# A decoder layer in single-precision split matmuls: how far weights are split ahead, where the gate job stands, how the first chunks and the last job are cut

## The chip, the core and the metric

The kernel runs on one core of a Trainium2 chip. A core has a matrix engine (TensorE, PE in the profile; its weight loads are shown apart as PEld), a vector engine (DVE), a scalar engine (ACT), a general engine (POOL) and SyncE (SP), which here issues nearly all transfers. Each engine works through its own list in order; semaphores hold an instruction until what it reads has been written. Accumulation goes to PSUM, everything else lies in SBUF, and transfers (DMA) run on 16 DMA engines. The metric is the device time of one execution in microseconds (us).

## The reference, cut to what matters

One decoder layer over 256 prompt tokens and 64 sample tokens (8 sequences of 8), 320 columns in all, with a model width of 2048:

```python
x = x + 0.5 * swiglu(rmsnorm(x, ln_ffa), w_ffa_in, w_ffa_out)      # d_ff 5632
x = x + token_mixer(rmsnorm(x, ln_mix), ...)
x = x + 0.5 * swiglu(rmsnorm(x, ln_ffb), w_ffb_in, w_ffb_out)
y = rmsnorm(x, ln_f)
# token_mixer: one projection h @ w_in gives mLSTM q/k (conv + SiLU), v, output gate, input/forget
# gates (8 columns: mif), attention q, k, v, and two branch gates;
# out = (sigmoid(gm) * (hm @ w_pm) + sigmoid(ga) * (ha @ w_pa)) @ w_out
```

`hm` is the mLSTM (chunked, with a running-max stabiliser) and `ha` the dilated attention over a cache of 2048 positions for the sample tokens. New keys, values and states are outputs too.

## The kernel before, in words

Activations are held transposed: a pair tile is 128 partitions x 2 x 320 columns, and eight pairs make one x. Each float32 operand of a large product is split into a high part, rounded to the matmul's format, and a low part, the rest. A product is three matmuls into the same PSUM tile: high weight x high activation, high weight x low activation, low weight x high activation.

The work is a list of jobs (`add_job`). A job makes 256 output columns and is cut into chunks of up to four 128-row blocks of the weight, 512 KB each; a full chunk is 2 halves of the columns x 4 blocks x 3 = 24 matmuls of 320 columns. There are 784 weight chunks and one gate chunk (`mif`, 16 blocks of 8 columns). A weight chunk goes through three steps: `load_upto` issues its transfer into one of RAWB raw buffers on SP; `split_upto` has ACT write the high part (`hi`, L223) and DVE the low part (`lo`, L224), into one of HLB pairs of buffers; PE uses it (L144, PSUM tile `fg`, two buffers). In chunk ci the kernel before splits up to chunk ci+2 (HLB 3) and issues loads up to chunk ci+6 (HLB + RAWB = 7 ahead, exclusive).

`run_job` (L270 on) writes the order of all engines out by hand. For each chunk: transfers that were put off (`run_later`), the split, then one step of each background generator (`even` and `odd` in alternate chunks, `slow` at 8 steps in 15 chunks, `every` in each), then, in a job's first chunk, its `setup` and `flush_evac`, which reads out the PSUM tile of the job before; then the loads, then the matmuls. Background generators are the attention over prompt (`prompt_attention`, even) and cache (`sample_attention`, slow), the `mlstm` (odd), the later parts of evacuations (every). Their small matmuls go to PSUM tile `bg` (four buffers) and stand in the PE list between chunks.

Stages: the first SwiGLU; the mixer projection: for p = 0..3 a job each for attention q, k, v, then `mif`, then per head mLSTM v (`mv`), two q/k jobs (`qk_evac`) and the output gate, then 16 gate jobs; then 8 jobs of `w_pm`, 8 of `w_pa`, 8 of `w_out`; the second SwiGLU. `mif_evac` (L801 on) computes log-sigmoids, scans and exponentials of 4-row tiles in nine steps of one chunk each. `mv_evac` scales its PSUM tile by rstd (L395) and two chunks later transposes it on PE (L332). `mlstm` loads q and k of head h+1 (`load_head`) after the fourth of four state steps of head h. The activations of `w_pm` (`hr`) and `w_pa` (`ar`) are four pair tiles; `presplit` splits the first of them during the job before, and `take` the others when the first job starts (L1301, L1302).

At the start, x is loaded in four quarters of 512 columns and transposed on PE; `first_chunk` and `prep_pair` put these transposes, the gains (L1469) and the low parts (L1473) of two pairs ahead of, or between, the halves of the first chunks; `warm(8)` is filler matmuls. At the end, the last job is read out in `ffb_last`, squares are summed over rows by matmuls against ones (`token_sums`), the final norm's scale is made (L1582 to L1584), and Y is scaled in two halves of 1024 columns and stored by six transfers from SP.

Of the kernel before, what the change touches and what calls it, by code (L numbers as in the profile page):

```python
# [128 lines left out]
def decoder_kernel(tc, I, O, K):  # L129
# [55 lines left out]
    RAWB, HLB, KRB = 4, 3, 3  # L185
# [219 lines left out]
    xl = {}  # L405

    def load_x(c):
        xl[c] = fp.tile([128, 3, 512], F32, tag="xl", bufs=3, name="xl")
        G.memset(xl[c][64:128, 2], 0.0)
        dma(xl[c][:, 0:2], I["x_prompt"][0].rearrange("(t p) d -> p t d", p=128)[:, :, c * 512:(c + 1) * 512])  # L410
        dma(xl[c][0:NS, 2], I["x_sample"].rearrange("b t d -> (b t) d")[:, c * 512:(c + 1) * 512])
# [194 lines left out]
    def sample_attention():  # L606
# [145 lines left out]
        for u in range(17):  # L752
# [51 lines left out]
    def mif_evac(ps):  # L804
# [5 lines left out]
        rst = mp_tile("rst")[0:4, :, 0:NT]  # L810
# [156 lines left out]
    def mlstm():  # L967
# [313 lines left out]
    add_job(w_in, 0, 16, C_MIF, mov_x, mif_evac, kind="mif")  # L1281
# [25 lines left out]
    def presplit(key):  # L1307
        while key not in M:
            yield
        PRE[key] = split_act(M[key][0], t_tile)  # L1310

    def take(key):
        for h in range(4):
            BH[h], BL[h] = PRE[key] if h == 0 and key in PRE else split_act(M[key][h], t_tile)
# [83 lines left out]
    def token_sums(x):  # L1398
        ps = bg_tile()
        for t, t0 in enumerate(TOK):  # L1400
            for m in range(2):
                mm(ps[:, t:t + 1], x[:, m, t0:t0 + 128], ones[:, 0:1], m == 0, m == 1)
        return ps


    def ffb_last(ps, j):
# [3 lines left out]
        if j < 7:  # L1410
            V.scalar_tensor_tensor(X[j], ps[:, :, 0:NT], 0.5, X[j], op0=OP.mult, op1=OP.add)
            sumsq(X[j], j, p)
        else:
            Y["sq"] = ft_tile("sq")
            for m in range(2):
                V.scalar_tensor_tensor(X[j][:, m], ps[:, m, 0:NT], 0.5, X[j][:, m], op0=OP.mult, op1=OP.add)
                S.activation(Y["sq"][:, m], X[j][:, m], AF.Square)
# [5 lines left out]
        if j < 7:  # L1423
            yield
        if j == 6:
            pa_ = token_sums(state["ss"])
            V.tensor_copy(rt, pa_[:, 0:3])
# [25 lines left out]
    vps = bg_tile()  # L1453
    tr(vps[:, 0:16], vffa)
    V.tensor_copy(gv[:, 0:16], vps[:, 0:16])

    def prep_pair(j, fg=False):
# [3 lines left out]
        ft = fg_tile() if fg else None  # L1461
        ps = [ft[:, 0], ft[:, 1]] if fg else [bg_tile(), bg_tile()]
# [4 lines left out]
        V.tensor_copy(X[j][:, 1], ps[1][:, 0:NT])  # L1467
        for m in range(2):
            S.activation(XH[j][:, m], ps[m][:, 0:NT], AF.Copy, scale=gv[:, g0 + m:g0 + m + 1])  # L1469
            if m == 0:  # L1470
                S.copy(X[j][:, 0], ps[0][:, 0:NT])
# [4 lines left out]
    def first_chunk(n, m):  # L1476
        if n == 0 and m == 0:
# [5 lines left out]
        elif n < 3:  # L1483
            prep_pair(2 * n + 2 + m)
            if m == 1:
                split_upto(n + 2)
        elif m == 0:
            split_upto(n + 2)

    def vec_table():  # L1490
        for _ in range(4):
# [6 lines left out]
    def first_sumsq():  # L1498
        for c in ((), (), (0,), (1, 2), (3, 4, 5), (6, 7)):
# [3 lines left out]
        rstd_now()  # L1503

    def init_tables():
        yield
# [68 lines left out]
    for job in jobs:  # L1575
        run_job(job)
    run_later()


    flush_evac()  # L1580
    pb_ = token_sums(Y["sq"])
    V.tensor_tensor(rt, rt, pb_[:, 0:3], op=OP.add)  # L1582
# [5 lines left out]
    for c in range(2):  # L1588
        if c:
            drain()  # L1590
        for t in range(3):
            r0 = 0 if t < 2 else 64
            a = yt[r0:128, t, c * 1024:(c + 1) * 1024]
            if t == 1:
                S.activation(a, a, AF.Copy, scale=rt[r0:128, t:t + 1])
            else:
                V.tensor_scalar(a, a, rt[r0:128, t:t + 1], None, op0=OP.mult)  # L1597
            dma((ypv[:, t] if t < 2 else ysv)[:, c * 1024:(c + 1) * 1024], a)
# [34 lines left out]
```

## Time and profile before

| | |
|---|---|
| median of 3 runs | 2980.31 us (2979.14 to 2981.5) |
| profiled execution's own time | 2975.59 us |
| its span, first to last instruction | 2973.8 us |
| PE busy | 2924.8 us (98%) |
| DVE / ACT / POOL busy | 1637.5 / 1087.8 / 226.0 us |
| read from and written to memory | 521.58 MB, 32.28 MB |

The span covers the instructions; the profiled time is 1.8 us more. A matmul's end is modelled, so the PE's busy time holds a little pipeline overlap. Windows give busy time for stretches of the span, with the clock that was granted to TensorE (1.00 is full speed) and the mean share of the DMA engines; waits name the instruction or transfer that ended an engine's idle time.

### The profile page before, as it was taken

The page shows a single profiled execution, that of the slowest core. Times are in us where ns is not written, and L with a number is a line of the kernel's source. Part 1 is how long each engine was busy: PE and PEld are TensorE (multiplying, and loading weights), DVE is VectorE, ACT ScalarE, POOL GpSimd, SP SyncE. Part 2 cuts the span into 40 slices and gives each one's busy share as a digit, 9 for nine tenths or more (in the row PEclk, how much of TensorE's full clock was granted, in tenths as well). Part 3 has the DMA queues.
Part 4 walks back from the last instruction along what each step waited for, and adds up shares of the span by engine and source line. Part 5 has one row for each costly group of instructions (what it writes and reads, how often), then busy time and mean ns, then how long its engine had stood idle before and what let it go on. Part 6 is the DMA issues. An engine that isn't in the chain of part 4 may idle for free.

```text
span 2973.8 us, 51323 instructions
## 1 busy us (share of the span) xinstructions
PE 2924.8 (98%) x21538; PEld 2875.4 (97%) x21538; DVE 1637.5 (55%) x1939; ACT 1087.8 (37%) x1359; POOL 226.0 (8%) x256
## 2 busy tenths in 40 slices
PE   9999999999999999999999999999999999999998
PEld 8999999999999999988889999999999999999998
DVE  6444444444446556878888875654444444444444
ACT  5332333333334333433443443334333333333334
POOL 1000000000000000122222210000000000000000
PEclk9999999999999999999999999999999999999999
DMA  6454444444546788898999986554444444445443
GB/s 195 151 159 155 149 149 149 149 150 143 158 145 184 224 231 248 223 296 272 301 282 313 308 275 218 184 176 152 150 149 149 149 149 150 151 146 156 149 141 115
DMA packets 507477, 557.23 MB, mean 187 GB/s; under 512 B 30125, under 2 KB 452061, under 8 KB 507221
## 3 DMA queue, kind: packets, MB, share of 16 engines
q1 hardware_dynamic: 507068, 553.87, 61.2%
q8 instruction: 169, 2.77, 0.4%
q14 instruction: 64, 0.52, 0.1%
q10 hardware_dynamic: 176, 0.07, 0.0%
HBM read 521.58 MB, written 32.28 MB: 186 GB/s over the span
## 4 chain that ended last, share of the span: by engine, by line
PE 50%; DMA 1%; DVE 1%; issue 0%; ACT 0%; DVEq 0%; SPq 0%; ACTq 0%
PE fg L144 47%; PE bg L144 3%; PE bg L332 0%; DMA raw<-in_w_in_dram 0%; DMA vt<-in_cache_v_dram 0%; DMA k<-qk_d 0%; DMA raw<-in_w_pm_dram 0%; DVE kd L631 0%; DVE lo L224 0%; DVE pre L928 0%; ACT hi L223 0%; DVE sg L958 0%; DVE vs L1073 0%; DVE Y L1597 0%; DVE bl L1302 0%
## 5 line engine op out<-in xcount | busy, mean ns | idle before, releaser
L224 DVE TENSOR_TENSOR lo<-raw,hi 128x1024 fp32r<-128x1024 f32 (+1 forms) x784 | 969.1, 1237 | 1204.2 <-ACT hi L223 1189.9
L144 PE MATMUL fg<-xh,hi 128*128 128x320 f32 x4240 | 1323.0, 312 | 2.6 <-ACT hi L223 2.6
L144 PE MATMUL fg<-xh,lo 128*128 128x320 f32 x4240 | 1314.3, 310 | 8.6 <-DVE lo L224 8.6
L144 PE MATMUL fg<-xl,hi 128*128 128x320 f32 x4240 | 1313.0, 310 | 0.0
L223 ACT CAST hi<-raw 128x1024 fp32r<-128x1024 f32 (+1 forms) x784 | 806.3, 1029 | 1356.7 <-PE fg L144 1014.2
L144 PEld LDWEIGHTS fg<-xh,lo 128*128 128x128 f32 x4240 | 797.4, 188 | 11.7 <-DVE lo L224 11.5
L144 PEld LDWEIGHTS fg<-xh,hi 128*128 128x128 f32 x4240 | 797.9, 188 | 5.7 <-ACT hi L223 3.1
L144 PEld LDWEIGHTS fg<-xl,hi 128*128 128x128 f32 x4240 | 797.8, 188 | 1.0 <-issue 0.2
L144 PE MATMUL fg<-hh,hi 128*128 128x320 f32 x1408 | 437.0, 310 | 0.0
L144 PE MATMUL fg<-hl,hi 128*128 128x320 f32 x1408 | 435.2, 309 | 0.0
L144 PE MATMUL fg<-hh,lo 128*128 128x320 f32 x1408 | 435.2, 309 | 0.0
L144 PEld LDWEIGHTS fg<-hl,hi 128*128 128x128 f32 x1408 | 264.4, 188 | 0.7 <-issue 0.7
L144 PEld LDWEIGHTS fg<-hh,hi 128*128 128x128 f32 x1408 | 264.4, 188 | 0.7 <-issue 0.7
L144 PEld LDWEIGHTS fg<-hh,lo 128*128 128x128 f32 x1408 | 264.4, 188 | 0.0
L439 POOL TENSOR_TENSOR gt<-gt,rstd 128x640 f32<-128x640 f32 x44 | 69.2, 1573 | 1876.8 <-ACT gt L438 1876.8
L144 PE MATMUL fg<-bl,hi 128*128 128x320 f32 x512 | 158.5, 310 | 1.9 <-DVE bl L1302 1.9
L144 PE MATMUL fg<-bh,hi 128*128 128x320 f32 x512 | 158.7, 310 | 1.5 <-ACT bh L1301 1.5
L144 PE MATMUL fg<-bh,lo 128*128 128x320 f32 x512 | 158.3, 309 | 0.0
L631 DVE STREAM_TRANSPOSE kd<-kraw 128x512 f32<-128x512 f32 x160 | 101.2, 677 | 10.8 <-DMA kraw<-in_cache_k_dram 10.8
L144 PEld LDWEIGHTS fg<-bl,hi 128*128 128x128 f32 x512 | 96.1, 188 | 2.4 <-DVE bl L1302 2.4
L144 PEld LDWEIGHTS fg<-bh,hi 128*128 128x128 f32 x512 | 96.1, 188 | 2.2 <-ACT bh L1301 2.0
L144 PEld LDWEIGHTS fg<-bh,lo 128*128 128x128 f32 x512 | 96.1, 188 | 0.0
(295 smaller groups left out, 1495.7 us busy)
## 6 DMA issues: line engine op xcount, KB each, us to landing
raw<-in_w_ffa_in_dram SPq DMA_DIRECT2D x176, 512.0 KB
raw<-in_w_in_dram SPq DMA_DIRECT2D x176, 512.0 KB
raw<-in_w_ffb_in_dram SPq DMA_DIRECT2D x176, 512.0 KB
raw<-in_w_ffa_out_dram SPq DMA_DIRECT2D x80, 512.0 KB
raw<-in_w_ffb_out_dram SPq DMA_DIRECT2D x80, 512.0 KB
kraw<-in_cache_k_dram SPq DMA_DIRECT2D x96, 256.0 KB
vt<-in_cache_v_dram SPq DMA_DIRECT2D x128, 192.0 KB
kraw<-in_cache_k_dram SPq DMA_DIRECT2D x32, 512.0 KB
```

What stands on the lines that cost most here:

```text
L144: T.matmul(out, a, b, start=start, stop=stop, **kw)
L223: S.copy(hi[:, :nk], t[:, :nk])
L224: V.tensor_tensor(lo[:, :nk], t[:, :nk], hi[:, :nk].bitcast(F32), op=OP.subtract)
L439: G.tensor_tensor(gt, gt, bcast(rstd, 2), op=OP.mult)
L631: V.transpose(kd[:, 2 * pr + g], t[:, g])
```

## The change

- Buffers: RAWB 4 to 3, HLB 3 to 4. In chunk ci the split now goes up to ci+3; loads still go up to ci+6.
- Order in a chunk: `setup` and the evacuation of the job before now stand ahead of the split and of the background steps.
- The `mif` job moves from behind the fourth attention triple to behind the first. Its tile `rst` comes from pool tag `m3` in place of `mp`.
- `load_head(h + 1)` after the third state step in place of the fourth. Two cache transposes of 512 columns become one of 1024. The tile of four attention outputs has one buffer in place of two.
- `presplit` splits two tiles, one per chunk, and `take` uses both.
- First four chunks: x and the first weight chunk arrive in halves, sample rows on ACT's queue; each pair is transposed, gained and split together with its half of the weight chunk, and its 12 matmuls follow (`first_chunk`); `warm(8)` is dropped; the sum of squares, table loads and vector loads move a few chunks later, `rstd_now` into chunk 6.
- Last job: `run_last` computes the two column halves one after the other, so the first half is read out under the second; the last 128 columns go from PSUM to Y scaled; the second store piece begins at column 1024 with 896 columns scaled in place, POOL scales the sample rows, and the middle store is issued by ACT.

```diff
-    RAWB, HLB, KRB = 4, 3, 3
+    RAWB, HLB, KRB = 3, 4, 3
...
             run_later()
-            if ci < 5:
-                first_chunk(ci, 0)
-            else:
+            if n == 0 and setup is not None:
+                setup()
+            if ci == 7 or (n == 0 and ci != 4):
+                flush_evac()
+            if ci > 3:
                 split_upto(ci + HLB)
...
             step(every)
-            if n == 0 and setup is not None:
-                setup()
-            if ci == 7 or (n == 0 and ci != 4):
-                flush_evac()
+            if ci < 4:
+                first_chunk(ci, ps)
+                load_upto(ci + 1 + RAWB)
+                continue
             load_upto(ci + HLB + RAWB)
...
-                if m and ci < 3:
-                    first_chunk(ci, 1)
+                if ci == 6 and m == 1:
+                    rstd_now()
...
-            for g in range(2):
-                V.transpose(kd[:, 2 * pr + g], t[:, g])
+            V.transpose(kd[:, 2 * pr:2 * pr + 2].rearrange("p a b -> p (a b)"), t.rearrange("p a b -> p (a b)"))
...
-                    o4 = mxt([128, 4, 128], "o", 2, "osb")
+                    o4 = mxt([128, 4, 128], "o", 1, "osb")
...
-        rst = mp_tile("rst")[0:4, :, 0:NT]
+        rst = m3_full("rst").rearrange("p a b -> p (a b)")[0:4, 0:2 * NT].rearrange("p (a n) -> p a n", a=2)
...
-                elif h < 3:
+                if s4 == 2 and h < 3:
                     while M["qk"] < 2 * (h + 2):
                         yield
                     load_head(h + 1)
...
-    add_job(w_in, 0, 16, C_MIF, mov_x, mif_evac, kind="mif")
+        if p == 0:
+            add_job(w_in, 0, 16, C_MIF, mov_x, mif_evac, kind="mif")
...
-        PRE[key] = split_act(M[key][0], t_tile)
+        for h in range(2):
+            PRE[key, h] = split_act(M[key][h], t_tile)
+            yield
...
+    def last_sum(ps, m):
+        p = pool_box["p"]
+        if m == 0:
+            Y["sq"], Y["xn"] = ft_tile("sq"), ft_tile("xn")
+        x, c = X[7][:, m], G_LF + 14 + m
+        V.scalar_tensor_tensor(x, ps[:, 0, 0:NT], 0.5, x, op0=OP.mult, op1=OP.add)
+        S.activation(Y["sq"][:, m], x, AF.Square)
+        S.activation(Y["xn"][:, m], x, AF.Copy, scale=gv[:, c:c + 1])
...
+    def run_last(job):
+        cs, nkt, mov, evac, kind, setup = job
+        for m in range(2):
+            ps = fg_tile()
+            for n, (ci, k0, nk) in enumerate(cs):
...
+                if m == 1 and n == 1:
+                    sp = token_sums([(state["ss"], 0), (state["ss"], 1), (Y["sq"], 0)])
+                    V.tensor_copy(rt, sp[:, 0:3])
+                    a = last_tr(0)
...
+            last_sum(ps, m)
...
-    for c in range(4):
-        load_x(c)
-        load_upto(c + 1)
-    load_vecs()
+    load_x(0, S)
+    load_x(1, S)
+    load_x(2, S)
+    raw[0] = wp.tile([128, 4, 256], F32, tag="raw", bufs=RAWB, name="raw")
+    for a in range(2):
+        load_xp(0, 256 * a, 256 * a + 256)
+        dma(raw[0][:, 2 * a:2 * a + 2], chunks[0][0][:, 2 * a:2 * a + 2])
...
+    def first_chunk(n, ps):
+        if n == 0:
             prep_pair(0)
             prep_pair(1)
-            split_upto(1)
-            prep_pair(2, True)
-            warm(8)
+        elif n == 3:
+            split_upto(5)
+        for pair in (2 * n, 2 * n + 1):
+            k0 = 2 * (pair % 2)
+            for which in range(3):
...
+            if pair < 6:
+                prep_pair(pair + 2)
+            elif pair == 6:
+                split_upto(6)
...
+    sp = token_sums([(Y["sq"], 1)])
+    a = last_tr(1)
...
+    drain()
+    for c0, c1, c2 in ((0, 1024, 1024), (1024, 1920, D)):
+        for t in (0, 1, 2):
...
+            if c2 > c1:
+                scale(y[:, c1:c2], a[r0:128, t * 128:(t + 1) * 128], S if t == 1 else V)
+            scale(y[:, c0:c1], y[:, c0:c1], (V, S, G)[t])
+            (S if t == 1 else nc.sync).dma_start((ypv[:, t] if t < 2 else ysv)[:, c0:c2], y[:, c0:c2])
```

More of the change, by code (lines that the diff above doesn't have):

```diff
@@ L1396, in decoder_kernel, with token_sums @@
     TOK = (0, 128, NT - 128)
-    def token_sums(x):
+    def token_sums(xs):
         ps = bg_tile()
         for t, t0 in enumerate(TOK):
-            for m in range(2):
-                mm(ps[:, t:t + 1], x[:, m, t0:t0 + 128], ones[:, 0:1], m == 0, m == 1)
+            for i, (x, m) in enumerate(xs):
+                mm(ps[:, t:t + 1], x[:, m, t0:t0 + 128], ones[:, 0:1], i == 0, i == len(xs) - 1)
         return ps
@@ L1409, in ffb_last @@
             S.activation(epst2, epst, AF.Sqrt)
[L1410 to L1417, printed above, removed]
+        V.scalar_tensor_tensor(X[j], ps[:, :, 0:NT], 0.5, X[j], op0=OP.mult, op1=OP.add)
+        sumsq(X[j], j, p)
         xn = ft_tile("xn")
@@ L1422, in ffb_last @@
         yield
[L1423 to L1427, printed above, removed]
+        yield
         a, b = bg_tile(), bg_tile()
@@ new lines, in last_tr @@
+    def last_tr(m):
+        xn, a = Y["xn"], bg_tile()
+        for t, t0 in enumerate(TOK):
+            tr(a[:, t * 128:(t + 1) * 128], xn[:, m, t0:t0 + 128])
+        return a
+    def run_last(job):
[3 more added lines that the diff above has]
+            for n, (ci, k0, nk) in enumerate(cs):
+                run_later()
+                split_upto(ci + HLB)
+                step(every)
+                if m == 0 and n == 0:
+                    flush_evac()
+                if m == 1 and n == 1:
+                    sp = token_sums([(state["ss"], 0), (state["ss"], 1), (Y["sq"], 0)])
+                    V.tensor_copy(rt, sp[:, 0:3])
+                    a = last_tr(0)
+                    S.copy(Y["t"][:, 0:2, 1792:1920], a[:, 0:256].rearrange("p (t c) -> p t c", t=2))
+                    V.tensor_copy(Y["t"][64:128, 2, 1792:1920], a[64:128, 256:384])
+                for k in range(nk):
+                    xh, xl = mov(k0 + k)
+                    c = slice(m * 128, (m + 1) * 128)
+                    first, last = k0 + k == 0, k0 + k == nkt - 1
+                    mm(ps[:, 0, 0:NT], wh[ci][:, k, c], xh, first, False)
+                    mm(ps[:, 0, 0:NT], wh[ci][:, k, c], xl, False, False)
+                    mm(ps[:, 0, 0:NT], wl[ci][:, k, c], xh, False, last)
+            last_sum(ps, m)
@@ L1444, in decoder_kernel @@
+    ff_jobs(I["w_ffb_in"][0], I["w_ffb_out"][0], lambda: pool_box["p"], ffb_last)
+    load_x(0, S)
[5 more added lines that the diff above has]
+        dma(raw[0][:, 2 * a:2 * a + 2], chunks[0][0][:, 2 * a:2 * a + 2])
+    st["loaded"] = 1
+    for c in (1, 2):
+        load_xp(c, 0, 512)
         load_upto(c + 1)
-    load_vecs()
+    load_upto(4)
+    load_x(3)
@@ L1452, in decoder_kernel, with split_half, gain_table, prep_pair @@
     warm(9)
[L1453 to L1457, printed above, removed]
+    def split_half(i, a):
+        if a == 0:
+            for d, nm in ((wh, "hi"), (wl, "lo")):
+                d[i] = wp.tile([128, 4, 256], F32R, tag=nm, bufs=HLB, name=nm)
+        r = slice(2 * a, 2 * a + 2)
+        S.copy(wh[i][:, r], raw[i][:, r])
+        V.tensor_tensor(wl[i][:, r], raw[i][:, r], wh[i][:, r].bitcast(F32), op=OP.subtract)
+        if a == 1:
+            raw.pop(i)
+            st["split"] = i + 1
+    def gain_table():
+        vps = bg_tile()
+        tr(vps[:, 0:16], vffa)
+        V.tensor_copy(gv[:, 0:16], vps[:, 0:16])
+    def prep_pair(j):
         xv, c0, g0 = xl[j // 2], (j % 2) * 256, G_FFA + 2 * j
@@ L1502, in first_sumsq @@
             yield
-        rstd_now()
     def init_tables():
-        yield
+        for _ in range(6):
+            yield
         tab = fp.tile([128, TABW], F32, name="tab")
@@ L1574, in decoder_kernel @@
     spawn(init_tables(), even)
-    for job in jobs:
+    for job in jobs[:-1]:
         run_job(job)
+    run_last(jobs[-1])
     run_later()
-    flush_evac()
-    pb_ = token_sums(Y["sq"])
-    V.tensor_tensor(rt, rt, pb_[:, 0:3], op=OP.add)
+    sp = token_sums([(Y["sq"], 1)])
+    a = last_tr(1)
+    V.tensor_tensor(rt, rt, sp[:, 0:3], op=OP.add)
     S.activation(rt, rt, AF.Sqrt, bias=epst, scale=1.0 / D)
```

60 lines of the change are left out of this document (32 added, 28 removed).

## The prediction

> **What bounds the kernel now.** I read the page first, then stretches of the span, then whom PE waited for where it was not full.
>
> ```profile
> span 2973.8 us, 51323 instructions
> PE 2924.8 (98%) x21538; PEld 2875.4 (97%) x21538; DVE 1637.5 (55%) x1939; ACT 1087.8 (37%) x1359; POOL 226.0 (8%) x256
> L224 DVE TENSOR_TENSOR lo<-raw,hi 128x1024 fp32r<-128x1024 f32 (+1 forms) x784 | 969.1, 1237 | 1204.2 <-ACT hi L223 1189.9
> L223 ACT CAST hi<-raw 128x1024 fp32r<-128x1024 f32 (+1 forms) x784 | 806.3, 1029 | 1356.7 <-PE fg L144 1014.2
> ```
>
> PE is busy for 98% of the span, and the change takes no product away. The 2973.8 - 2924.8 = 49 us of idle, and the time in which the clock was low, are all there is to win. A weight chunk costs ACT 1.03 and DVE 1.24 us. The stretches (from:to length, then busy time of PE, PEld, DVE, ACT, POOL, the granted clock, the DMA share, GB/s):
>
> ```profile
> 0.00:50.00 50.00, 43.20 (x275) 40.52 (x276) 32.20 (x45) 30.09 (x47) 2.39 (x10) 0.97 0.71 217
> 50.00:960.00 910.00, 910.00 (x6190) 905.86 (x6189) 415.44 (x393) 309.10 (x329) 39.71 (x33) 1.00 0.50 153
> 1010.00:1060.00 50.00, 50.00 (x351) 49.89 (x350) 24.81 (x39) 19.46 (x29) 0.00 (x0) 1.00 0.65 193
> 1180.00:1300.00 120.00, 112.45 (x1058) 106.70 (x1057) 93.59 (x174) 45.34 (x78) 15.83 (x29) 0.97 0.89 252
> 1300.00:1460.00 160.00, 147.58 (x1289) 135.99 (x1288) 132.74 (x210) 67.06 (x111) 45.10 (x64) 0.98 0.96 288
> 1460.00:1620.00 160.00, 157.19 (x1403) 148.42 (x1402) 142.17 (x201) 69.25 (x111) 43.79 (x53) 1.00 1.00 298
> 1620.00:1780.00 160.00, 156.73 (x1477) 147.88 (x1476) 128.49 (x170) 67.55 (x100) 34.57 (x38) 0.99 0.94 290
> 1780.00:1860.00 80.00, 76.61 (x594) 75.24 (x593) 47.04 (x47) 27.57 (x33) 2.93 (x2) 1.00 0.70 221
> 2955.00:2974.00 19.00, 6.54 (x52) 5.98 (x50) 5.25 (x11) 5.38 (x9) 0.00 (x0) 0.72 0.41 139
> ```
>
> The SwiGLU stretch from 50 to 960 has no idle: 910 us for 6190 matmuls, 0.147 us each. Nothing can be won there. Idle stands in four places: the start (6.8 us), the mixer from 1180 to 1780 (7.55 + 12.42 + 2.81 + 3.27 = 26.1), the change to `w_pm` and `w_pa` (3.4) and the end (12.5). In the mixer DVE is 78 to 89% busy, the DMA share is 0.89 to 1.00, and the low clock took 0.03 x 120 + 0.02 x 160 + 0.01 x 160 = 8.4 us more. PE's waits, from 1180 to 1780 and, the last two, from 1780 to 1860 (total, times, longest):
>
> ```profile
> PE fg L144 <- DVE lo L224: 6.7, 8, 2.4
> PE bg L332 <- DVE mv L395: 6.0, 3, 3.7
> PE bg L144 <- DMA k<-qk_d: 3.3, 1, 3.3
> PE bg L144 <- POOL ks L1021: 3.0, 3, 2.2
> ...
> PE fg L144 <- ACT hi L223: 2.3, 1, 2.3
> ...
> PE fg L144 <- DVE bl L1302: 1.9, 2, 1.0
> PE fg L144 <- ACT bh L1301: 1.5, 2, 0.7
> ```
>
> Weights come late for 6.7 + 2.3 = 9.0 us, but background products cost more: late `mv` and `ks`, and one late load of k.
>
> **The change part by part.** *Gate job and evacuation order.* The longest `mv` wait, with the busy time of the gate rows' instructions (DVE in the third place) ahead of it:
>
> ```profile
> 1160.00:1200.00 40.00, 0.00 (x0) 0.00 (x0) 10.17 (x24) 2.96 (x7) 0.39 (x1) 0.96 0.76 230
> ...
> 1191.45 0.82 DVE L395 TENSOR_TENSOR mv<-fg,rstd 128x640 f32<-128x640 f32 x1
> ...
> 1192.42 1.51 PE L332 MATMUL bg<-ident,mv 128*128 128x128 f32 x6 [3.68 <-DVE mv L395]
> ...
> 1194.53 0.47 PE L144 MATMUL fg<-xh,hi 128*128 128x320 f32 x1
> 1194.80 0.47 PE L144 MATMUL fg<-xl,hi 128*128 128x320 f32 x1
> ```
>
> `mv` was queued on DVE behind gate rows that take 10.17 us. After the wait PE ran at 0.27 us a matmul; for some six matmuls, and transposes at half rate too, I put that at 1.3 us. Behind the first attention triple the gate rows fall into 1010 to 1060, where DVE has 50 - 24.8 = 25 us free, so they fit; I keep 0.5 us for a wait there. Gain 3.7 + 1.3 - 0.5 = 4.5. The row transfers move along, into an SP list that is less crowded (share 0.65). Without that cover about 5 us of wait would only change its place.
>
> That evacuations stand first puts each split of a job's first chunk behind some 1 us on DVE, which the third chunk of lead (3.5 us) hides; without it the split would be that late. Costed at nothing.
>
> *q and k loaded one state step earlier.* The flights in the chain of waits that ended in PE's 3.3 us:
>
> ```profile
> 1596.53 9.68 DMA raw<-in_w_in_dram
> ...
> 1616.15 8.85 DMA k<-qk_d
> ```
>
> A state step is two steps of the odd list, four chunks, at least 4 x 3.5 = 14 us, more than the wait. The move takes six transfers (q, k, rows, scales, two of values) past the next head's other loads in SP's list; what is queued behind them has a state step of room. Gain 3.3 and the slow clock behind it, 1.3: 4.6. If the q/k jobs are not finished by then the generator only idles.
>
> *Two pieces split ahead.* The first chunk of each projection reads pieces 0 and 1, and only 0 was ready: 1.9 + 1.5 = 3.4 us. Pieces 2 and 3 are read a chunk later, and that chunk hides their splits (two of 0.7 on ACT and 0.8 on DVE, from the longest waits above and the ratio of 640 to 1024 columns). Gain 3.4, or none if no tile is free for the second piece.
>
> *Three chunks ahead, raw ring of three.* What is left of the mixer: 26.1 - 3.7 - 3.3 = 19.1 us of waits and 8.4 - 2.6 = 5.8 of slow clock, together 24.9. One more pair of split buffers gives each weight 3.5 us, and no weight wait was longer than 2.4. Against this stands why DVE was late. ACT's waits for weight transfers, and one of them:
>
> ```profile
> ACT hi L223 <- DMA raw<-in_w_in_dram: 48.3, 16, 9.0
> ...
> 1383.90 0.54 SPq L141 DMA_DIRECT2D raw<-in_w_in_dram  x1
> ...
> 1388.60 1.04 ACT L223 CAST hi<-raw 128x1024 fp32r<-128x1024 f32 x1 [7.95 <-DMA raw<-in_w_in_dram]
> ...
> 1300.00:1780.00 480.00, 120.76 (x98) 101.76 (x98) 0.99 0.97 292
> ```
>
> ACT and DVE stand still behind a weight that has not landed, and everything else they owe PE is late afterwards. With three raw buffers the load to split distance shrinks by a chunk, so they ask earlier and stand longer, while the total distance from load to matmul stays at six chunks. The new buffer therefore helps where DVE is late by its own work and does not help where the transfer is late. Bounds: all 24.9, or a loss of 10 (16 waits, each a chunk's 3.5 us earlier, 56 us of standing, of which DVE's idle share of 11 to 22% bears most and a fifth reaches PE). I take a third of the gain, 8 us, nearer to the middle, since weight waits are 9.0 of the 19.1.
>
> The joined cache transposes, the single `o` buffer and the `rst` tile cost nothing: the same columns, and about nine chunks between uses of `o`; without that room an ACT read-out would wait some chunks, on a slow generator.
>
> *The start.*
>
> ```profile
> 5.95 1.70 PE L332 MATMUL bg<-ident,xl 128*128 128x128 f32 x12
> ...
> 7.56 0.94 ACT L1469 ACTIVATE xh<-bg,gv 128x320 fp32r<-128x320 f32 x2
> ...
> 13.40 0.61 PE L144 MATMUL fg<-xh,hi 128*128 128x320 f32 x1
> 13.82 0.47 PE L144 MATMUL fg<-xl,hi 128*128 128x320 f32 x1
> ...
> 47.48 1.05 ACT L223 CAST hi<-raw 128x1024 fp32r<-128x1024 f32 x1 [2.44 <-PE fg L144]
> ```
>
> The first weight matmul came 7.5 us after the first transposes, behind two pairs, a whole split, a third pair and filler. Now it needs six transposes (0.85), two gains (0.94), half a split (0.6, half of 1.03 and a fixed part) and some 0.3 of hand-overs: 2.7 after 5.95, 8.6. From there to chunk 7, which began at 47.4, took 34.0 us; I add six transposes (0.7) and 0.6 for the clock, and take off 1.5 of the 6.8 idle, since a pair's gains and half split on ACT (0.94 + 0.6) now fit under its 12 matmuls (1.76) and 6 transposes. Chunk 7 begins at 8.6 + 33.8 = 42.4, 5.0 earlier. With the table's two transposes moved behind it (0.5 by these rates) I take 5.5. Bounds: 2 (first matmul at 11, waits kept) and 8.5 (no wait left).
>
> Dropping the filler is where a rule speaks against the change: the trace shows the first two matmuls 0.42 us apart behind the filler, and 0.27 after a 3.68 us wait. The Trainium skill (TensorE: Matmul & The Clock Gate, Part 1: The HAM clock gate) says that the clock starts at half, falls back after an idle window of about 3.4 us and needs about 3.4 us of sustained work to rise. By that rule, an estimate from its window, the slow phase would cost up to 1.7 us in place of my 0.6 and the start would gain 4.4. The trace's slow phase after `mv` agrees with the fall but was only some 2 us long.
>
> *The end.*
>
> ```profile
> 2959.23 0.89 DVE L1416 SCALAR_TENSOR_TENSOR x<-fg,x 128x320 f32<-128x320 f32 x2 [1.33 <-PE fg L144]
> ...
> 2960.34 1.64 PE L144 MATMUL bg<-ones,sq 128*128 128x1 f32 x12 [1.14 <-ACT sq L1417]
> ...
> 2967.74 1.30 SPq L141 DMA_DIRECT2D out_y_sample_dram<-Y  x1
> ...
> L439 POOL TENSOR_TENSOR gt<-gt,rstd 128x640 f32<-128x640 f32 x44 | 69.2, 1573 | 1876.8 <-ACT gt L438 1876.8
> ```
>
> After the last product one half instead of two is added and squared, and six instructions instead of twelve sum it: 0.4 + 0.8 less, some 0.8 with the waits. Inside the job PE gets 18 sums instead of 12 and three transposes more: 6 x 0.137 + 3 x 0.14 = 1.2 more. The 2.5 MB of stores follow as before; POOL's scaling of the sample rows is not in the trace: from 1.24 us, a DVE pass over 1024 columns, to 2.5, POOL's 1.57 for 640 columns scaled up. I take the upper end, POOL's own row; the last store waits for two of them, about as late as SP's last issue was. Together 0, between -2 and +2.
>
> *Sum.* 5.5 + 4.5 + 4.6 + 3.4 + 8 + 0 = 26 us. The profiled execution took 2975.59 us, 1.8 more than its span: 2949.6. The runs' median is 4.7 us above that execution: 2980.3 - 26 = 2954.
>
> **The rivals.**
> - *The lateness only moves.* The weights are in time, but ACT and DVE stand behind raw transfers a chunk sooner, so `mv`, `ks` and `qm` keep their waits and 3 us are added: 26 - 8 - 3 = 15, 2965. For it: the 48.3 us of ACT's waits. Against it: 9.0 us were waits for weights themselves.
> - *The mixer heals.* All 24.9 are won: 43, 2937. For it: no weight wait over 2.4. Against it: `ks`, `qm` and PSUM waits have other makers, and DVE is 89% busy in 1460 to 1620.
> - *The ring of three starves, and the kernel is slower.* A raw buffer's round is flight + cast + low part. With the 9.68 us flight it is (9.7 + 1.03 + 1.24) / 3 = 4.0 us a chunk (3.0 with four buffers); the stretch 1300 to 1780 used 480 / 98 = 4.9. It decides from a flight of 3 x 4.9 - 2.3 = 12.4 us on. At 13.4 the stretch grows by 0.33 x 98 = 33 us, less the 18 won elsewhere: 2995. For it: a share of 1.00. Against it: flights seen are below 10.
> - *The start does not do what it says.* The halves land no sooner and each pair waits for its split: 20.5 left, 2960.
>
> **How the numbers follow.** Forecast 45% (2946 to 2962), lateness moves 25%, mixer heals 15%, start fails 8%, ring starves 7%. A measurement here can tell about 0.2%, 6 us, from no change. The range 2937 to 2974 leaves out the starving ring, the tails of the healed mixer and of the moved lateness. Faster by over 0.2% (below 2974.3): all but the ring and 0.05 of the moved lateness, 0.88; within 0.2% 0.05; slower 0.07.
>
> **What would show it.** The first weight matmul near 8.6 and chunk 7 near 42; no wait on `bl`, `bh` or `k<-qk_d`; no `mv` wait near 1190 and none around 1010 to 1060; weight waits in the mixer near zero, with ACT's waits for `raw` above 48.3 us, perhaps twice that; SwiGLU stretches unchanged at 0.147 us a matmul; last product to last store within 2 us of before. I am wrong if PE's idle from 1180 to 1780 stays above 20 us, if waits for `lo` rise, or if idle appears from 50 to 960.

## The result and the profile after

The changed kernel takes 3014.4 us (median of 4 runs, 3010.0 to 3020.3), the kernel before 2979.9 us beside it: a ratio of 1.0116, with a 95% interval from 1.0094 to 1.0139. The forecast was 2954, within 2937 to 2974. The change costs 35 us where 26 were to be won. The profiled execution took 3010.39 us, its span 3008.6.

The same stretches as before (from:to length, then busy time of PE, PEld, DVE, ACT, POOL, the granted clock, the DMA share, GB/s):

```profile
0.00:50.00 50.00, 42.66 (x258) 40.43 (x259) 31.95 (x48) 29.92 (x52) 2.39 (x10) 0.93 0.63 191
50.00:960.00 910.00, 910.00 (x6189) 905.63 (x6188) 422.51 (x394) 308.80 (x330) 39.80 (x33) 1.00 0.48 154
...
1010.00:1060.00 50.00, 46.48 (x307) 45.48 (x306) 30.31 (x60) 20.71 (x34) 0.39 (x1) 0.93 0.52 150
...
1180.00:1300.00 120.00, 115.16 (x1001) 110.78 (x1003) 89.69 (x145) 41.00 (x70) 16.55 (x30) 0.97 0.92 271
1300.00:1460.00 160.00, 137.28 (x1185) 126.60 (x1177) 123.17 (x179) 63.23 (x104) 37.87 (x56) 0.90 0.87 261
1460.00:1620.00 160.00, 147.42 (x1405) 137.99 (x1403) 123.18 (x167) 63.40 (x103) 40.11 (x54) 0.96 0.90 270
1620.00:1780.00 160.00, 153.76 (x1338) 144.79 (x1337) 128.70 (x157) 64.94 (x100) 35.29 (x40) 0.97 0.94 282
1780.00:1860.00 80.00, 80.00 (x727) 78.22 (x726) 55.51 (x59) 28.64 (x37) 7.25 (x4) 1.00 0.82 257
```

The SwiGLU stretch is as it was: 910 us for 6189 matmuls. The loss lies in the mixer. From 1180 to 1780 PE idles 4.84 + 22.72 + 12.58 + 6.24 = 46.4 us, before 26.1. Read as the forecast read it, the clock column gives 0.03 x 120 + 0.10 x 160 + 0.04 x 160 + 0.03 x 160 = 30.8 us more, before 8.4. But a low clock costs time only while PE works, and now a good part of it falls on idle time. Two of the nine stretches at half clock (the first number behind the comma is PE's busy time):

```profile
1378.16:1384.98 6.82, 5.02 (x19) 5.02 (x20) 4.71 (x13) 4.12 (x9) 0.72 (x1) 0.50 1.02 278
1507.86:1514.69 6.83, 3.22 (x12) 3.22 (x13) 2.41 (x2) 2.96 (x5) 1.46 (x2) 0.50 1.04 322
```

The nine last 61.4 us and hold 41.5 us of PE's work, so the low clock cost half of that, 20.7 us. Before, five such stretches of 17.1 us held 16.6 us of work, 8.3 us. Idle and low clock together took 20.3 + 12.4 = 33 us more in this part of the mixer. From 960 to 1180 idle rose from 0.3 to 5.6 us, and from 1780 to 1860 it fell from 3.4 to 0.

The DMA share went down, not up, where it had been 0.96 and 1.00: the transfers are spread over a longer time. The waits from 1180 to 1780 (engine, tile waited with, who ended it; total, times, longest):

```profile
ACT hi L223 <- DMA raw<-in_w_in_dram: 93.4, 27, 8.4
...
PE bg L144 <- POOL ks L1026: 20.9, 4, 8.3
ACT isb L1119 <- DMA out_C_sample_dram<-C: 20.2, 2, 10.5
...
PE bg L144 <- ACT kw L1082: 11.4, 2, 7.3
...
PE bg L334 <- DVE mv L397: 5.6, 2, 4.8
```

No wait of PE for `hi` or `lo` is left there: the weights are in time, as the fourth pair of buffers promised. What comes late are the background operands `ks`, `kw` and `mv`. ACT's waits for raw transfers went from 42.5 us (14 times) in this stretch to 93.4 (27 times), and there is a wait that the kernel before did not have: the read-out `isb`, which waits for a store of C. ACT around the longest wait of PE, and PE's own row:

```profile
1497.65 1.06 ACT L223 CAST hi<-raw 128x1024 fp32r<-128x1024 f32 x1 [2.56 <-DMA raw<-in_w_in_dram]
1509.25 0.37 ACT L1119 COPY isb<-bg 128x256 f32<-128x256 f32 x1 [10.54 <-DMA out_C_sample_dram<-C]
1509.52 0.51 ACT L1024 ACTIVATE ks<-kr,eb 128x256 fp32r<-128x256 f32 x1
```

```profile
1511.47 0.80 PE L144 MATMUL bg<-vs,ks 128*128 128x256 f32 x2 [8.27 <-POOL ks L1026]
```

ACT does its list in order, so `ks`, half a microsecond of work, stands 10.5 us behind `isb`, and PE stands 8.3 us behind `ks`, with finished weights beside it.

### The profile page after: what moved, and what is told of

The parts are those of the page before. It is cut to its first block, busy times and chain, and to the rows that moved or that the text cites. A ratio compares the mean times of both kernels' runs of the same rounds, so it can differ in the third digit from the quotient of the medians.

```text
span 3008.6 us, 51344 instructions
## 1 busy us (share of the span) xinstructions
PE 2935.5 (98%) x21522; PEld 2886.9 (96%) x21522; DVE 1644.8 (55%) x1863; ACT 1084.4 (36%) x1364; POOL 227.1 (8%) x258
## 4 chain that ended last, share of the span: by engine, by line
PE 86%; issue 4%; DMA 4%; DVE 3%; ACT 1%; SPq 0%; POOL 0%; POOLq 0%; ACTq 0%; DVEq 0%
PE fg L144 81%; PE bg L144 4%; DMA raw<-in_w_in_dram 2%; DVE lo L224 1%; PE bg L334 1%; ACT hi L223 1%; DMA vt<-in_cache_v_dram 1%; DVE kd L636 0%; DVE y L925 0%; DMA kraw<-in_cache_k_dram 0%; DVE pre L933 0%; DMA out_C_sample_dram<-C 0%; SPq L141 0%; DMA C<-in_state_C_dram 0%; DVE sg L963 0%
## 5 line engine op out<-in xcount | busy, mean ns | idle before, releaser
L636 DVE STREAM_TRANSPOSE kd<-kraw 128x1024 f32<-128x1024 f32 x80 | 96.3, 1218 | 0.7 <-DMA kraw<-in_cache_k_dram 0.7
```

Source lines behind the costliest of these rows:

```text
L636: V.transpose(kd[:, 2 * pr:2 * pr + 2].rearrange("p a b -> p (a b)"), t.rearrange("p a b -> p (a b)"))
```

## The experiments

From the two readings came two theories of the loss: the shorter raw ring (A) and the earlier head load (B), with the order of a chunk and the gate job as what neither covers (C; later D, for the order alone). The times below, but for the changed kernel's own, were measured beside runs of the kernel before on the same chip, whose medians were 2976.7 to 2978.5 us; the ratios are to those runs.

**Ring and head load, undone one at a time and together.** Ring back, in the changed kernel:

```diff
-    RAWB, HLB, KRB = 3, 4, 3
+    RAWB, HLB, KRB = 4, 3, 3
```

> The changed kernel with the weight ring as before: four raw buffers and three pairs of split buffers (split two chunks ahead); all other parts as changed. Theory A (the ring of three makes ACT, and DVE behind it, stand behind transfers that have not landed, and ks, kw, qm and mv come late): ACT's waits for raw from 1180 to 1780 fall from 93 to about 45 us, PE's idle there from 46 to about 25 us, the time to 2975 to 2990. Theory B (the earlier load of the next head's q and k puts the read-out isb behind a store of C, 9.7 and 10.5 us on ACT): the two isb waits stay, and with them PE's waits for ks of 4.6 and 8.4 us; the time falls by less than 10, to 3004 or more. Theory C (the order of a chunk or the gate job): below 5 us of change.

Head load back:

```diff
-                if s4 == 2 and h < 3:
+                elif h < 3:
                     while M["qk"] < 2 * (h + 2):
```

> The changed kernel with the next head's q, k, rows, scales and values loaded one state step later, as before; ring of three kept. Theory B: the isb waits on the store of C (20.2 us of ACT, two) go, PE's waits for ks of 4.6 and 8.4 us and the slow clock behind them go; the wait for k (3.3) comes back: 10 to 16 us faster, 2998 to 3004. Theory A: raw waits of ACT stay near 93 us in the mixer and PE's idle above 38 us; within 6 us of 3014. Theory C: no change.

The kernel before with the ring alone (`RAWB, HLB = 3, 4`, and one `o` buffer instead of two for the space):

> The kernel before with only the weight ring changed: three raw buffers, four pairs of split buffers, and the single o buffer that makes room for them. Theory A: slower than before by 15 to 25 us (2995 to 3005), ACT's waits for raw in the mixer about 90 instead of 42.5 us, weight waits of PE in the mixer gone. Theories B and C: within 6 us of before, or faster by up to the 9 us of weight waits, 2971 to 2986.

Ring and head load both back:

> The changed kernel with the ring as before and the load of the next head one state step later as before. Theories A and B together: the mixer's idle falls to 25 us or less; what is left of the loss is the gate job's place (3.7 us wait at 1040 and the low clock of 1010 to 1060, 3.5 us) against the gains of the start and the presplit pieces (8 us): 2970 to 2980. Theory C (order of a chunk, gate job) holding most of the loss: above 2990.

| kernel | us | ratio | 95% interval |
|---|---|---|---|
| changed | 3014.4 | 1.0116 | 1.0094 to 1.0139 |
| changed, ring back | 2981.5 | 1.0019 | 1.0008 to 1.0030 |
| changed, head load back | 3000.6 | 1.0076 | 1.0058 to 1.0094 |
| before, ring of three | 3008.8 | 1.0103 | 1.0085 to 1.0122 |
| changed, ring and head load back | 2976.5 | 0.9993 | 0.9984 to 1.0003 |

0.001 is 3 us. The ring alone costs 0.0103 in the kernel before (31 us) and 0.0097 (29 us) in the changed one; the first is more than the 15 to 25 us that I had expected of theory A. Putting the head load back wins 0.0040 (12 us) with the ring of three and 0.0026 (8 us) with the ring of four. With the ring alone in the kernel before, PE's waits for `lo` and `hi` in the mixer go too, and ACT's for raw come:

```profile
ACT hi L223 <- DMA raw<-in_w_in_dram: 117.5, 35, 11.8
```

The two losses keep their own signs in the traces from 1180 to 1780. With the head load alone back, ACT has no `isb` wait and its raw waits stay at 104.2 us. With the ring alone back, the raw waits are 31.8 us, but `isb` still waits 9.4 us for the store of C and PE 24.0 us for `ks`, so PE's idle falls only to 36.3 us, not to the 25 that I had expected of theory A.

So theory A holds for most of the loss and theory B for a part. What neither explains is the last row: ring and head load are back, and the kernel is only at the level of before.

**What else is in it.** Starting from ring and head load back (2976.5 us), the order of a chunk, the gate job, and both, as before; and the order alone in the kernel before:

```diff
-            if n == 0 and setup is not None:
-                setup()
-            if ci == 7 or (n == 0 and ci != 4):
-                flush_evac()
             if ci > 3:
                 split_upto(ci + HLB)
 ...
             step(every)
+            if n == 0 and setup is not None:
+                setup()
+            if ci == 7 or (n == 0 and ci != 4):
+                flush_evac()
```

> Ring and load of the next head as before (as in the run of 2976.5 us), and now the order of a chunk as before too: split, generators, setup, evacuation. Theory D: with the evacuation first, its generator is stepped a second time in the same chunk, so what it gives PE (sums for rstd, transposes of mv) is listed one chunk sooner, while its inputs queue as before. Then the waits of PE for ss (2.2 us near 962 and 1.8 near 2026) and for kw fall away: 5 to 12 us faster than 2976.5. Rival: the order costs nothing, within 4 us of 2976.5.

```diff
-        if p == 0:
-            add_job(w_in, 0, 16, C_MIF, mov_x, mif_evac, kind="mif")
+    add_job(w_in, 0, 16, C_MIF, mov_x, mif_evac, kind="mif")
 ...
-        rst = m3_full("rst").rearrange(...)
+        rst = mp_tile("rst")[0:4, :, 0:NT]
```

> Ring and load of the next head as before, and the gate job at its old place behind the fourth attention triple, its row constants in their old buffer; order of a chunk as changed. Theory: at its new place it makes late weights and probabilities from 1010 to 1060 (PE busy 47.3 of 50 us, before 50), at its old place it makes mv late near 1190 (3.7 us and slow clock), so the two are near each other: within 4 us of 2976.5. Rival: the new place is dear (buffers and rows also in the heads' way): 5 or more faster. Forecast's view: 4.5 slower.

> Ring, load of the next head, order of a chunk and gate job all as before; what stays is the pairwise start, the split last job, two presplit pieces, the joined cache transposes and the single o buffer. If only the mixer parts lose: 2978 less 2.6 (chunk 7 starts some 2.6 us sooner by the run with the old ring) less 3.4 (no wait for bl and bh) = 2972, between 2968 and 2975. Rival: the joined transposes or the single o buffer cost too, 2976 or more.

> The kernel before with only the order of a chunk changed: setup and evacuation first, then split, then generators. Theory D: waits for ss near 965 and 2030 of about 2 us each appear, mv waits grow, weights come later behind the evacuation: 3 to 10 us slower than before. Rival: within 3 us of before, or faster because evacuations free their accumulators sooner.

| kernel (ring four and three, head load as before) | us | ratio | 95% interval |
|---|---|---|---|
| order as changed, gate job moved | 2976.5 | 0.9993 | 0.9984 to 1.0003 |
| order as before, gate job moved | 2968.9 | 0.9967 | 0.9954 to 0.9979 |
| order as changed, gate job as before | 2978.5 | 0.9998 | 0.9989 to 1.0007 |
| both as before | 2974.1 | 0.9981 | 0.9971 to 0.9991 |
| the kernel before, order as changed | 2983.7 | 1.0021 | 1.0013 to 1.0030 |

The order costs 0.0026 (8 us) in the one base and 0.0021 (6 us) in the other: theory D's size in both. Its sign in the trace is the sum for rstd behind the first SwiGLU. PE's wait for it from 960 to 1180 in the kernel before with the new order, and then in the kernel before as it was:

```profile
PE bg L144 <- DVE ss L381: 2.0, 1, 2.0
```

```profile
PE bg L144 <- DVE ss L381: 0.3, 1, 0.3
```

`flush_evac` steps the evacuation's generator once and appends it to `every`; where `step(every)` follows in the same chunk, it is stepped again at once. What it gives PE is listed a chunk sooner, while DVE's work for it is not done sooner. A second such sum, behind the mixer, waits 1.7 us instead of 0.2. The two sums are some 3 of the 6 us; where the rest of it arises was not traced.

The kernel with both as before keeps the single `o` buffer and the joined cache transposes, and at 2974.1 us it lies where it was expected without a price for them. So neither shows a cost, and the single `o` buffer does not explain the run of the kernel before with the ring of three.

The gate job's move is worth 0.0014 (4 us) with the old order, near the limit of what can be told: the two intervals overlap. With the new order it wins nothing that can be told. PE's waits for `mv` from 1180 to 1300 with the gate job at its old place, and at its new one (old order both):

```profile
PE bg L334 <- DVE mv L397: 3.9, 2, 3.5
```

```profile
PE bg L334 <- DVE mv L397: 0.4, 1, 0.4
```

**The ring taken apart**, on the kernel of 2968.9 us: raw buffers and pairs three and three, three and four, five and three; and the early head load without its value tile (`vq`, which shares nine buffers with C and `isb`).

> The kernel of 2968.9 us (ring four and three, head load and order as before, gate job moved) with the raw ring cut to three and the split buffers left at three: the split stays two chunks ahead, a load stands three chunks ahead of its split instead of four. Theory A1 (what costs is the shorter distance from load to split; ACT stands behind the transfer whatever the lead of the split): ACT's waits for raw in the mixer rise from 50 to 90 or more, 20 to 32 us slower, 2989 to 3001. Theory A2 (what costs is asking for the split a chunk earlier): within 8 us of 2968.9.

> The same kernel with three raw buffers and four pairs of split buffers, split three chunks ahead. Both theories: 20 to 32 us slower than 2968.9. A1: within 8 us of the run with three and three (the fourth pair neither helps nor hurts by more); A2: the whole loss appears only here.

> The same kernel with five raw buffers and three pairs (the space that the single o buffer and the unused rest leave). Theory A1: one chunk more from load to split: ACT's waits for raw in the mixer fall from 50 to 20 us or less, waits of PE for lo, hi, ks and mv there (about 20 us) fall by a third or more: 4 to 12 us faster, 2957 to 2965. Rival: the loads that start earlier take their transfer time from keys, values and k, and PE waits for these: within 4 us of 2968.9 or slower.

```diff
                 elif h < 3:
+                    load_vq(h + 1)
+                if s4 == 2 and h < 3:
                     while M["qk"] < 2 * (h + 2):
                         yield
                     load_head(h + 1)
```

> The same kernel with q, k, rows and scales of the next head loaded one state step earlier, but the values that share their buffers with C and isb loaded at the old step. Theory B: the isb waits on the store of C came from that one buffer taken earlier, so no isb wait appears here, and PE's wait for k (1.1 in this kernel) goes: 0 to 4 us faster than 2968.9. Rival: the early transfers themselves hurt (crowded transfers, list of SP): slower by 3 or more.

| raw buffers, pairs | us | ratio | 95% interval | ACT's waits for raw, 1180 to 1780 |
|---|---|---|---|---|
| 4, 3 | 2968.9 | 0.9967 | 0.9954 to 0.9979 | 49.7 us, 15 times |
| 3, 3 | 2991.8 | 1.0049 | 1.0034 to 1.0065 | 126.0, 38 |
| 3, 4 | 2999.1 | 1.0069 | 1.0055 to 1.0083 | 135.8, 39 |
| 5, 3 | 2967.2 | 0.9969 | 0.9958 to 0.9979 | 3.8, 1 |
| 4, 3, early head without `vq` | 2968.2 | 0.9969 | 0.9957 to 0.9980 | 64.0, 19 |

The third raw buffer less is what costs: 0.0082 (24 us) with the split where it was. The fourth pair adds 0.0020 (6 us) to that, with intervals that overlap a little; it wins nothing in this one pair of runs that differ in it alone, though PE's waits for `hi` and `lo` from 1180 to 1780 go from 10.8 us to none. Theory A1 stands in this direction. In the other its price was wrong: a fifth raw buffer takes ACT's waits for raw from 49.7 to 3.8 us and the time does not move; PE's idle from 1180 to 1780 is 22.5 us, with four buffers 21.0. And the early head load, without `vq`, shows no `isb` wait and no wait of PE for k in the mixer, and is neither faster nor slower: theory B holds for the buffer, and the 4.6 us were not there.

**Why the ring costs.** Two light kernels, on the same base with four and with three raw buffers, leave out the value transfers of the cached attention behind its first unit:

```diff
             hg, b = divmod(u, 8)
+            if u:
+                VT[u, pc] = VT[0, pc]
+                return
             t = mxt([128, 2, 512], "v4", 6, "vt")
```

> The kernel of 2968.9 us with the value transfers of the sample attention left out for all units but the first (their products read the first unit's values), some 28 of the 140 MB that move from 1300 to 1780; raw ring of four, three pairs of split buffers. The output of the sample attention is not the reference's. It is the base for the next run: transfers land sooner, ACT's waits for raw fall from 50 to 25 us or less, 2960 to 2969 us.

> The same light kernel with a raw ring of three. It too leaves those value transfers out. Theory A1 (the shorter ring costs because the transfer has not landed when ACT comes to it, and it lands late because the transfers are full): with a fifth of the traffic gone the ring of three costs less than half of the 23 us it costs with the whole traffic: under 10 us above the light kernel with four, ACT's waits for raw under 70 us instead of 126. Rival (the ring costs by its order: SP's list waits for a free raw buffer, and everything behind it in that list, keys, C, k, comes later whatever the traffic): still 18 us or more above the light kernel with four.

They take 2951.3 us (0.9915, interval 0.9900 to 0.9929) and 2955.0 us (0.9930, 0.9913 to 0.9947). The shorter ring costs 0.0015 here, with intervals that overlap, and 0.0082 with the whole traffic. The stretch from 1180 to 1780 and ACT's wait for raw, first with the whole traffic and three raw buffers, then light and three:

```profile
1180.00:1780.00 600.00, 568.37 (x5125) 530.69 (x5124) 476.82 (x660) 240.00 (x385) 135.22 (x182) 0.97 0.92 277
ACT hi L223 <- DMA raw<-in_w_in_dram: 126.0, 38, 11.7
```

```profile
1180.00:1780.00 600.00, 587.10 (x5420) 553.94 (x5419) 499.94 (x683) 253.76 (x402) 141.04 (x184) 0.99 0.78 232
ACT hi L223 <- DMA raw<-in_w_in_dram: 35.0, 10, 10.6
```

With the share at 0.78 ACT finds a transfer that has not landed 10 times instead of 38. The rival, that SP's list behind a raw buffer that is not free costs by itself, needed 18 us and finds 4, so most of the price of the shorter ring hangs on the traffic. The light kernel with four won more than I had expected (2951 against 2960 to 2969). One caution: the light kernels also spare whatever the value transfers cost in waits of their own.

**A version that beats both**: five raw buffers, early head load without `vq`, old order, gate job moved, and the new start, end and presplit pieces.

> The kernel of 2968.9 us with five raw buffers and with q, k, rows and scales of the next head one state step earlier, its values at the old step (the two runs of 2967.2 and 2968.2 us together). If each takes away a wait of its own: 2963 to 2967. If ACT's waits for raw are worth nothing below some 50 us and k's wait returns through crowding: 2966 to 2970.

2966.6 us, 0.9967 (0.9954 to 0.9980). It is no better than the 2968.9 of the simpler kernel that has four buffers and the old head load; the interval of each holds the other. What wins 0.33% over before is the start, the pieces and, near the limit of what can be told, the gate job's place.

## Why the prediction was wrong, step by step

Undone one after the other, the parts divide the loss like this: ring 0.0097, head load 0.0026, order 0.0026, and the rest -0.0033, together 0.0116. They add up because each is the step to the next kernel; in another order the sizes differ (the head load is 0.0040 with the ring of three).

*What bounds the kernel.* Right place: the SwiGLU did not move and the mixer decided. But I priced idle time with a small addition for the clock. The change made 20 us more idle in the mixer, and the low clock cost 12 us more.

*Three chunks ahead, raw ring of three: +8 forecast, 29 to 31 us lost.* This is the step that failed, and its lower bound of -10 with it. I had the mechanism in the text (ACT and DVE stand still behind a weight that has not landed, and what they owe PE comes late) and the observable right: no weight wait in the mixer, and ACT's raw waits about twice as long. Two things in the bound were wrong. It lengthened the 16 waits that were there (14 of them from 1180 to 1780), while 27 to 39 appear in that stretch: transfers that had just been in time no longer are. And it let a fifth of the standing time reach PE. In the kernel before with the ring of three ACT stood 117.5 - 42.5 = 75 us longer and the kernel lost 31 us: 0.4. Some of that was outside the mixer, at a place I had not looked at; PE's waits from 0 to 50 in that kernel and in the kernel before:

```profile
PE bg L144 <- DVE ss L377: 6.6, 1, 6.6
```

```profile
PE bg L144 <- DVE ss L377: 0.5, 1, 0.5
```

In the runs that take the ring apart, this part does not come with the shorter raw ring but with the split that is asked for a chunk sooner. The same wait from 0 to 50 with three raw buffers and three pairs (2991.8 us), and with three and four (2999.1 us):

```profile
PE bg L144 <- DVE ss L379: 0.8, 1, 0.8
```

```profile
PE bg L144 <- DVE ss L379: 3.6, 1, 3.6
```

Chunk 7 begins at 44.3 in the one and at 48.4 in the other, so about 4 of the 6 us that the fourth pair adds are lost at the start. I had priced the ring in the mixer only.

I then took a value "nearer to the middle", since weight waits were 9.0 of the 19.1 us. That was the wrong quantity to go by: a weight wait that is cured hands PE on to the next late thing. Of the rivals, the starving ring had the sign, the place (full transfers) and nearly the size (33 us), but its mechanism did not happen: in the mixer of the changed kernel no weight was late for PE. The moved lateness had the mechanism, with a tenth of its price.

*q and k one state step earlier: +4.6 forecast, 8 to 12 us lost.* The wait for k went. I counted the six transfers in SP's list and not the buffers they are written to. The value tile takes one of nine buffers that C, `isb` and others share in turn; taken a step earlier, it puts `isb` behind a C whose store has not landed, 9.7 and 10.5 us, on ACT. With that tile alone at its old step (ring of four, old order) no `isb` wait is left, and the time is that of the old head load.

*Evacuations first: costed at nothing, 6 to 8 us lost.* I looked at where the split went and not at where the generators stand to the evacuation. My promised cover (three chunks of lead) was for the wrong instruction.

*Gate job: +4.5 forecast, about 4 us won* with the old order, and the wait for `mv` went. In the changed kernel PE waits for the prompt attention's scores, in the stretch that I had said had room; from 960 to 1180:

```profile
PE bg L334 <- DVE s L577: 3.5, 1, 3.5
```

With the ring alone put back this wait is 0.4 us, so the gate job's place is not enough to make it.

*Two pieces split ahead: +3.4.* No wait for `bl` or `bh` is left in the changed kernel. With the old order two waits of 0.7 and 1.0 us, at `w_pa`, remain.

*The start: first matmul right, gain lost behind it.* The first weight matmul comes at 9.12 (forecast 8.6), but chunk 7 begins where it did before. PE's rows of the changed kernel at the start and at the sum for rstd, in the middle of chunk 6:

```profile
9.12 1.21 PE L144 MATMUL fg<-xh,hi 128*128 128x320 f32 x4 [0.61 <-ACT hi L1506]
10.13 1.27 PE L144 MATMUL fg<-xl,hi 128*128 128x320 f32 x4
11.20 1.27 PE L144 MATMUL fg<-xh,lo 128*128 128x320 f32 x4
12.27 1.09 PE L334 MATMUL bg<-ident,xl 128*128 128x128 f32 x6
13.12 0.83 PE L144 MATMUL fg<-xh,hi 128*128 128x320 f32 x4
...
42.79 1.74 PE L144 MATMUL bg<-ss,ones 128*128 128x320 f32 x4 [3.57 <-DVE ss L379]
...
47.28 0.30 PE L144 MATMUL fg<-xh,hi 128*128 128x320 f32 x1
```

The row at 47.28 is the first of chunk 7 (the thirteenth behind the sum); before it was 47.4. The sum of squares came 3.6 us late and left a slow phase. With the ring alone put back the wait is 0.6 us. With ring, head load and order as before:

```profile
40.44 1.31 PE L144 MATMUL bg<-ss,ones 128*128 128x320 f32 x4 [0.59 <-DVE ss L379]
41.35 0.55 PE L144 MATMUL fg<-xh,hi 128*128 128x320 f32 x1
...
41.73 0.31 PE L144 MATMUL fg<-xl,hi 128*128 128x320 f32 x1
```

Eleven steps of 0.147 behind 41.73 chunk 7 begins at 43.3: 4.1 us earlier, of the 5.0 forecast. Of the two prices for the slow phase the rule's was the better one: the first 12 matmuls took 12.27 - 9.12 = 3.15 us instead of 12 x 0.147 = 1.76, and the six transposes 0.85 instead of some 0.58, together 1.7 us more; I had 0.6. The Trainium skill (TensorE: Matmul & The Clock Gate, Part 1: The HAM clock gate) asks for about 3.4 us of sustained work before the clock rises; the trace agrees: the half clock lasts from 9.41 to 12.83, 3.4 us. The slow phase behind `mv` in the kernel before, which I had put at some 2 us, was 2.9 us of PE's work, from 1192.42 to 1195.33.

*The end: 0 forecast, about 0 measured.* From the last product to the end of the span it is 13.3 us, before 14.6. But the sums and transposes that moved into the job stand ahead of the last product: from the 240th last product to the end it is 53.6 us, before 53.9.

Start, pieces and end together, without the mixer parts, are worth 0.0019 (6 us), for 8.9 forecast.

What stays open: how much of the light kernels' 16 us (0.9967 to 0.9915) is due to transfers of weights and how much to the left-out transfers' own waits, and whether a fourth pair of split buffers beside four raw ones would win anything. It wants 4 KB a partition more than three and four, or five and three, and was not tried. Open too is why ACT's waits that the fifth buffer took away were worth nothing, and how the ring's 24 us divide over the late operands.

## What to carry to other kernels

Where engines work through their lists in order, price a shorter transfer ring by what is queued behind the instruction that waits for it, not by the consumer's own wait; if transfers are near full, many of those that are just in time can miss. When an allocation or a generator step moves by one place, follow the shared buffers in their turn and the number of steps per chunk as carefully as the queues. A deeper ring need not win: here a fifth buffer took the consumer's waits away and the time stayed.

## What was not expected of the hardware

A wait of PE cost more than its length. Behind the 4.5 us wait for `ks`, matmuls came every 0.27 us from 1380 until 1384.8; behind the 8.3 us wait until 1514.7, 3.2 us:

```profile
1379.96 0.80 PE L144 MATMUL bg<-vs,ks 128*128 128x256 f32 x2 [4.49 <-POOL ks L1026]
1380.56 0.47 PE L144 MATMUL fg<-xh,hi 128*128 128x320 f32 x1
1380.83 0.47 PE L144 MATMUL fg<-xl,hi 128*128 128x320 f32 x1
...
1384.56 0.47 PE L144 MATMUL fg<-xh,hi 128*128 128x320 f32 x1
1384.83 0.39 PE L144 MATMUL fg<-xl,hi 128*128 128x320 f32 x1
1385.05 0.31 PE L144 MATMUL fg<-xh,lo 128*128 128x320 f32 x1
```

The phase behind the shorter wait loses 2 us by itself (16 matmuls from 1380.56 to 1384.83, 4.27 us, for 16 x 0.147 = 2.35), and from 1180 to 1780 the low clock cost 0.45 us for each microsecond of idle (20.7 for 46.4; before 8.3 for 26.1, where most waits were short). A longer wait did not cost more in this way, because the first part of the half clock fell on the wait itself: 1.8 us behind the 4.5 us wait, 3.6 us behind the 8.3 us wait.

Shorter waits lower the clock too. In the kernel before, PE waited 2.4 us for one `lo`, until 1286.75. The 3.4 us around that wait, and the 3.4 us that follow:

```profile
1284.09:1287.50 3.41, 1.01 (x7) 0.75 (x6) 3.18 (x7) 0.00 (x0) 0.00 (x0) 1.00 1.07 300
1287.50:1290.91 3.41, 3.41 (x15) 3.41 (x14) 1.28 (x5) 2.34 (x4) 0.62 (x4) 0.50 0.95 267
```

PE worked 1.0 us of the first and paid with half clock in the whole of the second. The Trainium skill (TensorE: Matmul & The Clock Gate, Part 1: The HAM clock gate), by which the prediction let the clock fall after an idle window of about 3.4 us, differs here: a wait of 2.4 us was enough.

The other surprise is that leaving out a fifth of the transfers in the mixer won 16 us, while taking ACT's waits for transfers away with a fifth buffer won none.
